# Gate and value products of w_up: one 512-column and one 256-column matmul, folded afterwards, with padded operand rows

## The chip, the cores and the metric

The kernel runs on one core of a Trainium2 chip. The metric is the device time of one execution in microseconds (us). The kernel before takes 1085.06 us, the median of three runs (1084.09 to 1086.23). One execution was recorded by the hardware profiler; the views of that profile are what the prediction argues from.

## The reference

One layer of a streaming encoder on x of shape (1, 256, 2048), all in float32:

```
h = RMSNorm(x);  u = h @ w_in                       # 2048 x 4352
y = concat(short gated conv, Conformer conv (31 taps, LayerNorm), multi-scale pooling)
x = x + RMSNorm(y @ w_out)                          # 2048 x 2048
h = RMSNorm(x)
g, v = causal_conv3(h @ w_up) + bias                # 2048 x 11264, split in two halves of 5632
x = x + RMSNorm((silu(g) * v) @ w_down)             # 5632 x 2048
```

The convolutions run over the 256 tokens, per channel, looking back only.

## The kernel before, in words

**Layout.** Channels lie on the 128 partitions and the T = 256 tokens along the free axis, so that an activation of 2048 channels is KD = 16 row blocks k of 128 x 256. The weights stay in HBM as 364 units of 128 x 1024 floats (68 of w_in, 32 of w_out, 176 of w_up, 88 of w_down), read in one stream by `load` (line 99) into four buffers `raw`.

**Two-part products.** Every operand is split into a high part in the type fp32r and a low part, the rest. For weights, ScalarE copies `raw` to `whi` (`split_hi`, line 108), and VectorE subtracts to get `wlo` (`split_lo`, line 114); each has five buffers. The function `ahead(i)` issues these splits up to AHEAD = 4 units in front of unit i. For activations, `h1`, `y_t` and `h2` have the shape [128, 16, 2, 256]: for each k the 256 high columns, then the 256 low ones, so that one k takes 2,048 bytes of a partition. A product of a weight block with row block k (`product`, line 242) is three matmuls of 256 columns into the same PSUM region: whi with the high part, whi with the low part, wlo with the high part.

**Stages.** In order: the products of w_in with h1 (tiles named in, in_head, in_pool, in_cv, in_b), beside which the mixers run on VectorE, ScalarE and GpSimd (the 31 taps are `acc`, line 379); those of w_out with y_t (tiles o); the second norm, woven into the first products of w_up (tiles up); the rest of w_up (tiles gv); and w_down (tiles d), where the activation parts g_hi and g_lo are the stationary operand and 512 columns of whi or wlo are the moving one (lines 749 to 751).

**Column pairs.** `mm_pair` makes two output columns of 128 channels, one after the other, into the two halves of one PSUM bank: four units, 16 k each, 96 matmuls. In w_up the pair is a gate column j and its value column KF + j, of 44 pairs. The first four pairs come from `mm_group`, which takes eight columns at once along k (tiles up0 to up3, `first[0]` to `first[3]`); the other forty are gv4 to gv43. The PSUM pool has six buffers of one bank.

**The gate.** `gate(j, ps)` scales a pair by the token scale `r2_bc` (VectorE, line 710, PSUM to the SBUF tile `u`), runs the three-tap convolution of each half (`conv3`: ScalarE line 701, VectorE line 703 twice), SiLU on ScalarE (line 712), the product on GpSimd (line 714), and splits the result into g_hi (ScalarE, line 715) and g_lo (VectorE, line 716). Gates 0 to 3 are issued together between the two columns of gv4, gate 4 after gv4, and so on; after gv4 a 128 x 1024 transpose of x follows on VectorE (`transpose_blocks`, line 684).

**Order of the work.** `tick()` counts units; `later(n, fn)` runs fn n units on. The token scales of the second norm come that way: `scales` one unit after the up group, `r2_bc` one more. Each engine works its queue in order. The order within a queue follows the order of the program where operands and buffers allow it, as the framework's own schedule reckons; some instructions are pinned to program order.

**Sum of squares.** In the up stage `square_sum` squares two row blocks at once on ScalarE (line 300), and GpSimd adds the 512 columns to `sum_2` (line 302); small matmuls (line 218) then reduce its two halves over partitions.

Of the kernel before, what the change touches and what calls it, by code (L numbers as in the profile page):

```python
# [8 lines left out]
F32 = mybir.dt.float32  # L9
# [50 lines left out]
UP_ORDER = [x for j in range(KF) for x in (j, KF + j)]  # L60
NATURAL = list(range(KF))

AHEAD = 4
POOL_TAPS = 8

# [4 lines left out]
def trunk_kernel(ctx: ExitStack, tc, xt, vec, g_row, pool_w, w_in, w_out, w_up, w_down, out):  # L70
    nc = tc.nc
    const = ctx.enter_context(tc.tile_pool(name="const", bufs=1))
    units = ctx.enter_context(tc.tile_pool(name="units", bufs=5))
    psum = ctx.enter_context(tc.tile_pool(name="psum", bufs=6, space=bass.MemoryType.PSUM))
    psmall = ctx.enter_context(tc.tile_pool(name="psmall", bufs=2, space=bass.MemoryType.PSUM))
    stat = ctx.enter_context(tc.tile_pool(name="stat", bufs=2))

# [10 lines left out]
    def pin(ins, where=pinned):  # L88
        if where[0]:
            tc.keep_in_program_order(ins)  # L90
# [10 lines left out]
    def split_hi(i, pieces=1):  # L101
        if i not in raws:
            load(i)
        hi = units.tile([P, 1024], F32R, tag="whi", name=f"whi{i}")
        lo = units.tile([P, 1024], F32R, tag="wlo", name=f"wlo{i}")
        parts[i] = (hi, lo)
        for s in cut(pieces):
            pin(nc.scalar.activation(hi[:, s], raws[i][:, s], AF.Copy))  # L108
# [72 lines left out]
    table = const.tile([P, 1], F32, name="table")  # L181
    nc.scalar.activation(table, idle[:, :1], AF.Copy)

    def keep_busy(n):
        warm = psum.tile([P, 512], F32, tag="mm", name="warm")
        for _ in range(n):
            tc.keep_in_program_order(
                nc.tensor.matmul(  # L188
                    warm, idle, idle[:, None, :].to_broadcast([P, 4, P]), start=True, stop=True
                )  # L190
            )
# [3 lines left out]
    def v(name, i):  # L195
        return vec_sb[:, _AT[name] + i : _AT[name] + i + 1]
# [39 lines left out]

    def product(ps, w_hi, w_lo, h, first, last):
        terms = ((w_hi, h[:, 0]), (w_hi, h[:, 1]), (w_lo, h[:, 0]))  # L240
        for n, (w, x) in enumerate(terms):
            nc.tensor.matmul(  # L242
                ps, w, x, start=first and n == 0, stop=last and n == 2, skip_group_check=True
            )

    def bank(name):
        return psum.tile([P, 2, T], F32, tag="mm", name=name)

    def mm_column(u0, ps, ht, opens, order=NATURAL):
        for h in range(2):  # L250
            ahead(u0 + h)
            whi, wlo = parts.pop(u0 + h)
            for kk in range(8):
                k = 8 * h + kk
                c = slice(kk * P, (kk + 1) * P)
                product(ps, whi[:, c], wlo[:, c], ht[:, order[k]], opens and k == 0, k == KD - 1)
            tick()

    def mm_pair(u0, name, ht, order=NATURAL, between=None):
        ps = bank(name)  # L260
        mm_column(u0, ps[:, 0], ht, True, order)
        if between:
            between()
        mm_column(u0 + 2, ps[:, 1], ht, False, order)
        return ps

    def mm_group(u0, name, ht, n, before, order=NATURAL):


        pss = [bank(f"{name}{m}") for m in range(n // 2)]  # L270
        rows = 8 // n
        for u in range(KD // rows):
            for kk in range(rows):
                before(rows * u + kk)
            ahead(u0 + u)
            whi, wlo = parts.pop(u0 + u)
            for kk in range(rows):
                k = rows * u + kk
                for m in range(n):
                    c = slice((kk * n + m) * P, (kk * n + m + 1) * P)  # L280
                    product(
                        pss[m // 2][:, m % 2], whi[:, c], wlo[:, c], ht[:, order[k]],
                        k == 0 and m % 2 == 0, k == KD - 1,
                    )
            tick()
        return pss

    def twice(t):
        return t[:, None, :].to_broadcast([P, 2, T])


    with tc.tile_pool(name="mix", bufs=1) as mix, tc.tile_pool(name="mixt", bufs=2) as mixt:
        h1 = const.tile([P, KD, 2, T], F32R, tag="ht", name="h1")
        sum_x = mix.tile([P, 512], F32, tag="sum", name="sum_x")

        def square_sum(src, total, first, name):
            sq = total
            if not first:
                sq = mixt.tile([P, 512], F32, tag="sq", name=name)
            pin(nc.scalar.activation(sq, src, AF.Square))  # L300
            if not first:
                nc.gpsimd.tensor_tensor(total, total, sq, ALU.add)

        def two(t, kg):
            return t[:, 2 * kg : 2 * kg + 2].rearrange("p k t -> p (k t)")
# [31 lines left out]
        pin(nc.sync.dma_start(pw_sb, pool_w.rearrange("g c d -> c g d")), loading)  # L337
        loading[0] = False

        y_t = mix.tile([P, KD, 2, T], F32R, name="y_t")  # L340
        yo = mix.tile([P, KD, T], F32, name="yo")
        glu6 = mix.tile([P, N_HEADS, T], F32, name="glu6")
        acc6 = mix.tile([P, N_HEADS, 2, T], F32, name="acc6")
# [222 lines left out]
        def out_tiles(m, ps, n=2):  # L566
            sq = sum_y
            if m:
                sq = mixt.tile([P, 2, T], F32, tag="sq", name=f"sqy{m}")
            nc.scalar.activation(sq[:, :n], ps[:, :n], AF.Square)  # L570
            if m:
                nc.gpsimd.tensor_tensor(sum_y[:, :n], sum_y[:, :n], sq[:, :n], ALU.add)
            for j in range(n):
                nc.scalar.activation(
                    yo[:, m + j], ps[:, j], AF.Copy, scale=v("g_post", m + j)
                )
# [20 lines left out]
        for m in range(GROUP_OUT, KD - 2, 2):  # L597
            out_tiles(m, mm_pair(u0, f"o{m}", y_t, OUT_ORDER))
            u0 += 4

        ps = bank("o14")
        mm_column(u0, ps[:, 0], y_t, True, OUT_ORDER)
        out_tiles(KD - 2, ps, 1)
        later(1, most_squares)
        last = bank("o15")
        mm_column(u0 + 2, last[:, 0], y_t, True, OUT_ORDER)
        u0 += 4
        pinned[0] = True
        pin(nc.scalar.activation(last_sq, last[:, 0], AF.Square))
        m_y = stat.tile([P, 2], F32, tag="m2", name="m_y")  # L610
        ps = squares_by_token([last_sq], "y")
        pin(nc.vector.scalar_tensor_tensor(
# [5 lines left out]
        r_y = over_partitions(r, "y")  # L618
        keep_busy(8)
        ahead(u0)  # L620
        pin(nc.scalar.activation(yo[:, KD - 1], last[:, 0], AF.Copy, scale=v("g_post", KD - 1)))

        h2 = const.tile([P, KD, 2, T], F32R, tag="ht", name="h2")
        sum_2 = const.tile([P, 512], F32, name="sum_2")

        def scale_y(kg, ks=None):
            ks = ks or slice(2 * kg, 2 * kg + 2)
# [16 lines left out]
        def elementwise(k):  # L644

            kg, odd = divmod(k, 2)
            if k == 0:
                for j in range(2):
                    scale_y(0, slice(j, j + 1))
                    add_x(0, slice(j, j + 1))  # L650
                    make_lo(j, h2, "g_ffn")
            if not odd:
                if kg < 7:
                    scale_y(kg + 1)
                    add_x(kg + 1)
            else:
                if kg < 7:
                    parts_of(kg + 1)
                square_sum(two(xT, kg), sum_2, kg == 0, f"sq2{kg}")

        first = mm_group(u0, "up", h2, GROUP_UP, weave)
        u0 += 16
# [3 lines left out]
    with tc.tile_pool(name="ffn", bufs=1) as ffn, tc.tile_pool(name="ffnt", bufs=2) as ffnt:  # L666
# [4 lines left out]
        def scales():  # L671
            r_2 = token_rsqrt([sum_2], D, RMS_EPS, "x2")
            later(1, lambda: nc.scalar.activation(r2_bc, over_partitions(r_2, "x2"), AF.Copy))

        later(1, scales)


# [29 lines left out]

        def gate(j, ps):
            u = ffnt.tile([P, 2, T], F32, tag="u", name=f"u{j}")
            nc.vector.tensor_tensor(u, ps, twice(r2_bc), ALU.mult)  # L710
            a = conv3(u[:, 0], j, "cg")
            nc.scalar.activation(a, a, AF.Silu)  # L712
            b = conv3(u[:, 1], KF + j, "cv")
            nc.gpsimd.tensor_tensor(a, a, b, ALU.mult)  # L714
            nc.scalar.activation(g_hi[:, j], a, AF.Copy)
            nc.vector.tensor_tensor(g_lo[:, j], a, g_hi[:, j].bitcast(F32), ALU.subtract)

        n_first = GROUP_UP // 2
        for j in range(n_first, KF):
            ps = mm_pair(  # L720
                u0, f"gv{j}", h2,
                between=(lambda: [gate(i, first[i]) for i in range(n_first)])
                if j == n_first else None,
            )
            u0 += 4
            gate(j, ps)
            if 4 <= j < 28:
                c, at = divmod(j - 4, 6)
                if at == 0:
                    transpose_blocks(c)  # L730
                elif at < 5:
                    move_blocks(c, at - 1)
# [30 lines left out]
        n_kg = KF // 2  # L763
        tail = 4
        for nb in range(4):
            ps = [psum.tile([P, 512], F32, tag="mm", name=f"d{nb}{h}") for h in range(2)]
            for kg in range(n_kg - (tail if nb == 3 else 0)):
                mm_rows(u0 + nb * n_kg + kg, kg, ps)
            if nb < 3:
                for h in range(2):  # L770
                    square_block(nb, h, ps[h])
                    gain_block(nb, h, ps[h])
# [87 lines left out]
```

## Time and profile before

| | |
|---|---|
| median of three runs | 1085.06 us (1084.09 to 1086.23) |
| the profiled execution's own time | 1084.75 us |
| its span, first to last instruction | 1083.0 us, 19157 instructions |
| mean granted TensorE clock | 0.992 |
| DVE share of the span, ACT, POOL | 65%, 50%, 18% |
| HBM traffic over the span | 182 GB/s |

How to read the views: PE is TensorE's matmuls, PEld its weight loads, DVE is VectorE, ACT ScalarE, POOL GpSimd. In a group of instructions stand line, engine, operation, output<-inputs, shapes and count, then busy us and the mean ns of one, then the idle time before them and what ended it. In the chain in order of time stand start, length and what ran, with its count. In a timeline stand start, length, engine, line and operation; a bracket is the idle time before it. In windows, each engine's busy time (and count), then the granted TensorE clock, the DMA share and GB/s.

### The profile page before, as it was taken

How to read it: one execution, taken by the hardware profiler on the slowest of the kernel's cores; microseconds unless marked ns; L12 is line 12 of the kernel's file. 1: busy time of each engine (PE TensorE's matmuls, PEld its weight loads, DVE VectorE, ACT ScalarE, POOL GpSimd, SP SyncE). 2: the span in 40 equal slices, each digit the busy share in tenths (PEclk: the TensorE clock that was granted, in tenths of full speed). 3: DMA queues.
4: the chain of work that ended last, by engine and by line, in shares of the span. 5: the costliest groups of instructions: out<-in, count | busy, mean ns of one | idle time of the engine just before them, and what ended most of it. 6: DMA issues, size and time to landing. Idle time of an engine off the chain costs nothing.

```text
span 1083.0 us, 19157 instructions
## 1 busy us (share of the span) xinstructions
PE 1062.3 (98%) x7761; PEld 1007.5 (93%) x7761; DVE 708.5 (65%) x908; ACT 538.0 (50%) x740; POOL 192.4 (18%) x197
## 2 busy tenths in 40 slices
PE   9999999999999989999999999999999999999996
PEld 7999999999999979999999999999999888888885
DVE  7899988764467757566676766666666444444544
ACT  8745355465546545455454554554554343343431
POOL 4424446421113201011010111111111000000001
PEclk9999999999999989999999999999999999999999
DMA  8645555646545357375664755555556556655552
GB/s 287 202 155 177 179 178 194 208 157 208 185 152 179 116 151 238 115 242 189 174 234 123 250 194 184 185 182 187 179 188 220 193 177 193 193 183 188 193 176 77
DMA packets 73463, 200.00 MB, mean 185 GB/s; under 512 B 23712, under 2 KB 24480, under 8 KB 73248
## 3 DMA queue, kind: packets, MB, share of 16 engines
q1 hardware_dynamic: 73088, 197.72, 56.4%
q8 instruction: 60, 0.98, 0.4%
q10 hardware_dynamic: 288, 1.07, 0.3%
q14 instruction: 27, 0.22, 0.1%
HBM read 194.57 MB, written 2.10 MB: 182 GB/s over the span
## 4 chain that ended last, share of the span: by engine, by line
PE 91%; DVE 6%; issue 1%; ACT 1%; DMA 1%; SPq 0%; DVEq 0%; POOL 0%; ACTq 0%
PE gv L242 43%; PE o L242 8%; PE d L751 8%; PE d L749 8%; PE d L750 8%; PE in_cv L242 6%; PE up L242 4%; DVE acc L379 3%; PE in_b L242 3%; PE in L242 2%; DVE wlo L114 1%; PE in_head L242 1%; DMA raw<-in_w_in 0%; DMA xT<-in_xt 0%; PE warm L188 0%
## 5 line engine op out<-in xcount | busy, mean ns | idle before, releaser
L114 DVE TENSOR_TENSOR wlo<-raw,whi 128x1024 fp32r<-128x1024 f32 (+1 forms) x365 | 450.7, 1239 | 268.6 <-ACT whi L108 266.1
L108 ACT ACTIVATE whi<-raw 128x1024 fp32r<-128x1024 f32 (+1 forms) x365 | 382.7, 1054 | 388.5 <-PE d L751 134.1
L242 PE MATMUL gv<-h,whi 128*128 128x256 f32 x2560 | 463.7, 284 | 4.3 <-ACT whi L108 4.3
L242 PEld LDWEIGHTS gv<-h,whi 128*128 128x128 f32 x2560 | 401.5, 193 | 4.5 <-ACT whi L108 4.5
L242 PE MATMUL gv<-h,wlo 128*128 128x256 f32 x1280 | 363.6, 284 | 1.0 <-DVE wlo L114 1.0
L242 PEld LDWEIGHTS gv<-h,wlo 128*128 128x128 f32 x1280 | 247.1, 193 | 1.2 <-DVE wlo L114 1.2
L749 PE MATMUL d<-whi,g_hi 128*128 128x512 f32 x352 | 139.2, 396 | 0.0
L750 PE MATMUL d<-wlo,g_hi 128*128 128x512 f32 x352 | 139.2, 396 | 0.0
L751 PE MATMUL d<-whi,g_lo 128*128 128x512 f32 x352 | 139.2, 395 | 0.0
L714 POOL TENSOR_TENSOR cg<-cg,cv 128x256 f32<-128x256 f32 x44 | 57.6, 1309 | 413.1 <-ACT cg L712 406.5
L242 PE MATMUL o<-y_t,whi 128*128 128x256 f32 x512 | 91.0, 280 | 0.0
L749 PEld LDWEIGHTS d<-whi,g_hi 128*128 128x128 f32 x352 | 66.2, 188 | 15.9
L751 PEld LDWEIGHTS d<-whi,g_lo 128*128 128x128 f32 x352 | 66.2, 188 | 15.9
L750 PEld LDWEIGHTS d<-wlo,g_hi 128*128 128x128 f32 x352 | 66.2, 188 | 15.9
L242 PEld LDWEIGHTS o<-y_t,whi 128*128 128x128 f32 x512 | 78.2, 188 | 0.1
L242 PE MATMUL o<-y_t,wlo 128*128 128x256 f32 x256 | 71.5, 279 | 0.0
L242 PE MATMUL in_cv<-h,whi 128*128 128x256 f32 x384 | 69.8, 284 | 0.0
L379 DVE SCALAR_TENSOR_TENSOR acc<-glu,vec_sb,acc 128x246 f32<-128x246 f32 (+10 forms) x126 | 66.6, 569 | 2.5 <-POOL acc L402 2.2
L242 PEld LDWEIGHTS in_cv<-h,whi 128*128 128x128 f32 x384 | 60.0, 192 | 0.1
L242 PE MATMUL in_cv<-h,wlo 128*128 128x256 f32 x192 | 54.4, 283 | 0.2 <-DVE wlo L114 0.2
L242 PE MATMUL in_head<-h,whi 128*128 128x256 f32 x256 | 47.9, 289 | 0.0
L242 PEld LDWEIGHTS o<-y_t,wlo 128*128 128x128 f32 x256 | 47.9, 187 | 0.0
(140 smaller groups left out, 1114.7 us busy)
## 6 DMA issues: line engine op xcount, KB each, us to landing
raw<-in_w_up SPq DMA_DIRECT2D x176, 512.0 KB, 3.7
raw<-in_w_down SPq DMA_DIRECT2D x88, 512.0 KB, 4.2
raw<-in_w_in SPq DMA_DIRECT2D x67, 512.0 KB, 4.1
raw<-in_w_out SPq DMA_DIRECT2D x32, 512.0 KB, 4.2
xT<-blocks SPq DMA_DIRECT2D x64, 32.0 KB, 3.6
out<-tail_sb SPq DMA_DIRECT2D x8, 256.0 KB, 2.6
xT<-in_xt SPq DMA_DIRECT2D x7, 256.0 KB, 5.3
tail_sb<-in_g_row ACTq DMA_DIRECT2D x1, 1024.0 KB, 6.0
```

Of the source, the lines that this page charges most:

```text
L108: pin(nc.scalar.activation(hi[:, s], raws[i][:, s], AF.Copy))
L114: pin(nc.vector.tensor_tensor(lo[:, s], raw[:, s], hi[:, s].bitcast(F32), ALU.subtract))
L242: nc.tensor.matmul(ps, w, x, start=first and n == 0, stop=last and n == 2, skip_group_check=True)
L379: nc.vector.scalar_tensor_tensor(a[:, o:], glu[:, : T - o], cb(s), a[:, o:], ALU.mult, ALU.add)
L714: nc.gpsimd.tensor_tensor(a, a, b, ALU.mult)
L749: nc.tensor.matmul(pss[h], g_hi[:, k, s], w1, start=(k == 0), stop=False)
L750: nc.tensor.matmul(pss[h], g_hi[:, k, s], w2, start=False, stop=False)
L751: nc.tensor.matmul(pss[h], g_lo[:, k, s], w1, start=False, stop=(k == KF - 1))
```

## The change

1. *Fused product.* In the gv tiles, `wide_product` replaces the three matmuls of a k: one of 512 columns, whi with both parts of h2, and one of 256, wlo with the high part, into the first 256 columns. A column's sum so stands in two halves of 256 in a whole PSUM bank. The 512-column one comes first, except for the last k.
2. *Fold.* `gate` handles both banks of a gv tile at once: ScalarE copies the second halves (128 x 2 x 256) to `u`, VectorE adds the first halves, and a second VectorE instruction scales in SBUF. The tiles up0 to up3 keep the one scaling.
3. *PSUM.* Three buffers of two banks replace six of one. The two columns of a pair lie in two banks; up and o groups take two pairs per buffer; the last two columns of w_out share one buffer.
4. *First gates.* Gates 0 to 3 are issued 1, 2, 4 and 6 units after `scales`, gate 4 four units after gv4 and gate 5 one unit after gv5.
5. *Pads.* The rows of h1, h2 and y_t get 8 more floats (2,080 bytes instead of 2,048), and so do the buffers of whi and wlo (4,128 instead of 4,096).
6. *Sum of squares.* `sum_2` has 256 columns; GpSimd adds each row block by itself.

```diff
+PAD = 8
-    psum = ctx.enter_context(tc.tile_pool(name="psum", bufs=6, space=bass.MemoryType.PSUM))
+    psum = ctx.enter_context(tc.tile_pool(name="psum", bufs=3, space=bass.MemoryType.PSUM))
...
-        hi = units.tile([P, 1024], F32R, tag="whi", name=f"whi{i}")
-        lo = units.tile([P, 1024], F32R, tag="wlo", name=f"wlo{i}")
+        hi = units.tile([P, 1024 + PAD], F32R, tag="whi", name=f"whi{i}")[:, :1024]
+        lo = units.tile([P, 1024 + PAD], F32R, tag="wlo", name=f"wlo{i}")[:, :1024]
...
+    def banks(name):
+        return psum.tile([P, 2, 512], F32, tag="mm", name=name)
...
+    def wide_product(ps, w_hi, w_lo, h, opens, last):
+        def by_lo():
+            nc.tensor.matmul(ps[:, :T], w_lo, h[:, 0], start=False, stop=False)
+
+        if last:
+            by_lo()
+        nc.tensor.matmul(ps, w_hi, h, start=opens, stop=last)
+        if not last:
+            by_lo()
...
+    def mm_pair(u0, name, ht, order=NATURAL, between=None, wide=False):
+        ps = banks(name)
+        mm_column(u0, ps[:, 0], ht, order, wide)
         if between:
             between()
+        mm_column(u0 + 2, ps[:, 1], ht, order, wide)
+        return ps if wide else ps[:, :, :T]
...
+    def padded(pool, name, **kw):
+
+        t = pool.tile([P, KD, 2 * T + PAD], F32R, name=name, **kw)
+        return t[:, :, : 2 * T].rearrange("p k (j t) -> p k j t", j=2)
...
-        h1 = const.tile([P, KD, 2, T], F32R, tag="ht", name="h1")
+        h1 = padded(const, "h1", tag="ht")
...
-        y_t = mix.tile([P, KD, 2, T], F32R, name="y_t")
+        y_t = padded(mix, "y_t")
...
-        h2 = const.tile([P, KD, 2, T], F32R, tag="ht", name="h2")
-        sum_2 = const.tile([P, 512], F32, name="sum_2")
+        h2 = padded(const, "h2", tag="ht")
+        sum_2 = const.tile([P, T], F32, name="sum_2")
...
-                square_sum(two(xT, kg), sum_2, kg == 0, f"sq2{kg}")
+                sq = mixt.tile([P, 2, T], F32, tag="sq", name=f"sq2{kg}")
+                pin(nc.scalar.activation(sq, xT[:, 2 * kg : 2 * kg + 2], AF.Square))
+                for j in range(2):
+                    a = (sq[:, 0], sum_2)[kg > 0]
+                    if kg or j:
+                        nc.gpsimd.tensor_tensor(sum_2, a, sq[:, j], ALU.add)
...
             later(1, lambda: nc.scalar.activation(r2_bc, over_partitions(r_2, "x2"), AF.Copy))
+
+            for i, n in enumerate((1, 2, 4, 6)):
+                later(n, lambda i=i: gate(i, first[i]))
...
-            nc.vector.tensor_tensor(u, ps, twice(r2_bc), ALU.mult)
+            if ps.shape[-1] == T:
+                nc.vector.tensor_tensor(u, ps, twice(r2_bc), ALU.mult)
+            else:
+                nc.scalar.activation(u, ps[:, :, T:], AF.Copy)
+                nc.vector.tensor_tensor(u, ps[:, :, :T], u, ALU.add)
+                nc.vector.tensor_tensor(u, u, twice(r2_bc), ALU.mult)
...
-            ps = mm_pair(
-                u0, f"gv{j}", h2,
-                between=(lambda: [gate(i, first[i]) for i in range(n_first)])
-                if j == n_first else None,
-            )
+            ps = mm_pair(u0, f"gv{j}", h2, wide=True)
             u0 += 4
-            gate(j, ps)
+            if j == n_first:
+                later(4, lambda ps=ps: gate(n_first, ps))
+            elif j == n_first + 1:
+                later(1, lambda ps=ps: gate(n_first + 1, ps))
+            else:
+                gate(j, ps)
...
-            ps = [psum.tile([P, 512], F32, tag="mm", name=f"d{nb}{h}") for h in range(2)]
+            pair = banks(f"d{nb}")
+            ps = [pair[:, h] for h in range(2)]
```

More of the change, by code (lines that the diff above doesn't have):

```diff
@@ L182, in trunk_kernel @@
     nc.scalar.activation(table, idle[:, :1], AF.Copy)
+    def banks(name):
+        return psum.tile([P, 2, 512], F32, tag="mm", name=name)
     def keep_busy(n):
-        warm = psum.tile([P, 512], F32, tag="mm", name="warm")
+        warm = banks("warm")[:, 0]
         for _ in range(n):
@@ L235, in over_partitions, with product @@
         return ps[:, :T]
-    def product(ps, w_hi, w_lo, h, first, last):
+    def product(ps, w_hi, w_lo, h, opens, last):
         terms = ((w_hi, h[:, 0]), (w_hi, h[:, 1]), (w_lo, h[:, 0]))
@@ L242, in product, with mm_column @@
             nc.tensor.matmul(
-                ps, w, x, start=first and n == 0, stop=last and n == 2, skip_group_check=True
+                ps, w, x, start=opens and n == 0, stop=last and n == 2, skip_group_check=True
             )
-    def bank(name):
-        return psum.tile([P, 2, T], F32, tag="mm", name=name)
-    def mm_column(u0, ps, ht, opens, order=NATURAL):
+    def wide_product(ps, w_hi, w_lo, h, opens, last):
[6 more added lines that the diff above has]
+            by_lo()
+    def mm_column(u0, ps, ht, order=NATURAL, wide=False):
         for h in range(2):
@@ L255, in mm_column @@
                 c = slice(kk * P, (kk + 1) * P)
-                product(ps, whi[:, c], wlo[:, c], ht[:, order[k]], opens and k == 0, k == KD - 1)
+                args = (whi[:, c], wlo[:, c], ht[:, order[k]], k == 0, k == KD - 1)
+                if wide:
+                    wide_product(ps, *args)
+                else:
+                    product(ps[:, :T], *args)
             tick()
-    def mm_pair(u0, name, ht, order=NATURAL, between=None):
-        ps = bank(name)
-        mm_column(u0, ps[:, 0], ht, True, order)
+    def mm_pair(u0, name, ht, order=NATURAL, between=None, wide=False):
+        ps = banks(name)
+        mm_column(u0, ps[:, 0], ht, order, wide)
         if between:
             between()
-        mm_column(u0 + 2, ps[:, 1], ht, False, order)
-        return ps
+        mm_column(u0 + 2, ps[:, 1], ht, order, wide)
+        return ps if wide else ps[:, :, :T]
     def mm_group(u0, name, ht, n, before, order=NATURAL):
-        pss = [bank(f"{name}{m}") for m in range(n // 2)]
+        pss = []
+        for m in range(n // 4):
+            ps = banks(f"{name}{m}")
+            pss += [ps[:, j].rearrange("p (j t) -> p j t", j=2) for j in range(2)]
         rows = 8 // n
@@ L599, in trunk_kernel @@
             u0 += 4
-        ps = bank("o14")
-        mm_column(u0, ps[:, 0], y_t, True, OUT_ORDER)
-        out_tiles(KD - 2, ps, 1)
+        ps = banks("o14")
+        mm_column(u0, ps[:, 0], y_t, OUT_ORDER)
+        out_tiles(KD - 2, ps[:, :1, :T], 1)
         later(1, most_squares)
-        last = bank("o15")
-        mm_column(u0 + 2, last[:, 0], y_t, True, OUT_ORDER)
+        last = ps[:, 1, :T]
+        mm_column(u0 + 2, ps[:, 1], y_t, OUT_ORDER)
         u0 += 4
         pinned[0] = True
-        pin(nc.scalar.activation(last_sq, last[:, 0], AF.Square))
+        pin(nc.scalar.activation(last_sq, last, AF.Square))
         m_y = stat.tile([P, 2], F32, tag="m2", name="m_y")
@@ L620, in trunk_kernel @@
         ahead(u0)
-        pin(nc.scalar.activation(yo[:, KD - 1], last[:, 0], AF.Copy, scale=v("g_post", KD - 1)))
-        h2 = const.tile([P, KD, 2, T], F32R, tag="ht", name="h2")
-        sum_2 = const.tile([P, 512], F32, name="sum_2")
+        pin(nc.scalar.activation(yo[:, KD - 1], last, AF.Copy, scale=v("g_post", KD - 1)))
+        h2 = padded(const, "h2", tag="ht")
+        sum_2 = const.tile([P, T], F32, name="sum_2")
         def scale_y(kg, ks=None):
@@ L719, in trunk_kernel @@
         for j in range(n_first, KF):
-            ps = mm_pair(
-                u0, f"gv{j}", h2,
-                between=(lambda: [gate(i, first[i]) for i in range(n_first)])
-                if j == n_first else None,
-            )
-            u0 += 4
-            gate(j, ps)
+            ps = mm_pair(u0, f"gv{j}", h2, wide=True)
+            u0 += 4
+            if j == n_first:
+                later(4, lambda ps=ps: gate(n_first, ps))
+            elif j == n_first + 1:
+                later(1, lambda ps=ps: gate(n_first + 1, ps))
+            else:
+                gate(j, ps)
             if 4 <= j < 28:
```

## The prediction

> **What bounds the kernel now.** I read the page first: busy shares, the chain that ended last, the costliest groups.
>
> ```profile
> PE 1062.3 (98%) x7761; PEld 1007.5 (93%) x7761; DVE 708.5 (65%) x908; ACT 538.0 (50%) x740; POOL 192.4 (18%) x197
> PE 91%; DVE 6%; issue 1%; ACT 1%; DMA 1%; SPq 0%; DVEq 0%; POOL 0%; ACTq 0%
> L242 PE MATMUL gv<-h,whi 128*128 128x256 f32 x2560 | 463.7, 284 | 4.3 <-ACT whi L108 4.3
> L242 PE MATMUL gv<-h,wlo 128*128 128x256 f32 x1280 | 363.6, 284 | 1.0 <-DVE wlo L114 1.0
> L749 PE MATMUL d<-whi,g_hi 128*128 128x512 f32 x352 | 139.2, 396 | 0.0
> ```
>
> TensorE makes up 91% of the chain, and the gate and value tiles (gv) that the change rewrites are 3840 of its 7761 matmuls. The 284 ns of a record overlap the next record, so the price of a matmul is the distance between starts. The chain in order of time gives that as stretch divided by count:
>
> ```profile
> 144.64 23.04 PE in_cv L242 x192
> 234.87 69.61 PE o L242 x591
> 309.25 1.73 PE warm L188 x8
> 310.98 46.17 PE up L242 x384
> 360.02 0.79 PE ss_x L218 x8
> 387.38 440.41 PE gv L242 x3646
> ```
>
> A 256-column product costs 120.0 ns with h1 or h2 as the moving operand (23.04/192; up 46.17/384 = 120.2; gv 440.41/3646 = 120.8) and 117.8 ns with y_t (69.61/591). A bf16 512-column filler costs 216 ns (1.73/8). The only fp32r products of 512 columns are those of w_down; their timeline from 900 us, first and last of 23 consecutive starts:
>
> ```profile
> 899.72 0.40 PE L749 MATMUL d<-whi,g_hi 128*128 128x512 f32 x1
> ...
> 904.85 0.40 PE L750 MATMUL d<-wlo,g_hi 128*128 128x512 f32 x1
> ```
>
> 5.13 us over 22 steps is 233.2 ns. Next the gv stage (357 to 827 us) in windows:
>
> ```profile
> core 0: us, PE busy (x) PEld busy (x) DVE busy (x) ACT busy (x) POOL busy (x), PEclk, DMA share, GB/s
> 381.00:387.40 6.40, 1.03 (x8) 0.62 (x6) 5.05 (x8) 2.76 (x5) 1.74 (x2) 0.94 0.01 2
> 387.40:391.00 3.60, 3.60 (x17) 3.60 (x18) 2.09 (x3) 2.31 (x3) 0.51 (x1) 0.50 0.48 73
> 391.00:600.00 209.00, 209.00 (x1735) 209.00 (x1735) 137.31 (x182) 104.32 (x142) 22.37 (x17) 0.99 0.62 192
> 600.00:827.00 227.00, 227.00 (x1894) 227.00 (x1893) 151.28 (x199) 116.66 (x159) 28.42 (x20) 1.00 0.60 193
> ```
>
> From 391 us on TensorE never stops (1894 matmuls in 227 us, 119.9 ns each), so a shorter spacing shortens the stage one to one. The one hole lies at 381 to 387.4. VectorE's timeline shows its cause:
>
> ```profile
> 368.98 1.22 DVE L114 TENSOR_TENSOR wlo<-raw,whi 128x1024 fp32r<-128x1024 f32 x1
> 370.12 0.68 DVE L710 TENSOR_TENSOR u<-up,r_bc 128x512 f32<-128x512 f32 x1
> ...
> 384.58 1.24 DVE L684 STREAM_TRANSPOSE blocks<-xT 128x1024 f32<-128x1024 f32 x1
> ...
> 386.10 1.22 DVE L114 TENSOR_TENSOR wlo<-raw,whi 128x1024 fp32r<-128x1024 f32 x1
> ```
>
> Between 370.2 and 386.1 us VectorE runs gates 0 to 3 and the next ones back to back and not one weight split (wlo), so the lead of four units runs out. TensorE loses 6.40 - 1.03 = 5.4 us, and about 0.5 us more at the edges of what it did run. Then the granted clock is 0.50 for 3.6 us: 17 records where 3.6/0.120 = 30 would fit, and with the missing records counted I take 2.4 us. Together about 8.3 us.
>
> **Fused product.** Per product, three matmuls of 256 columns (360 ns) become one of 512 and one of 256; the columns streamed stay 768, one weight load of three goes. There are 40 tiles x 2 columns x 16 k = 1280 products. Nearest rows: 233.2 for the wide one, 117.8 to 120 for the narrow one; I take 118: rows of h are 2,048 bytes and weight buffers 4,096 apart, and in the layout before they all start at one place modulo 512 bytes (y_t 320 bytes off it); with the pads they spread in steps of 32. Pair 351.2, saving 8.8 ns, times 1280 = **-11.3 us**, all on the path. Bounds: nothing, if the wide one costs 2 x 120; and the filler's rate, 216 + 108 = 324, which gives -46 us.
>
> **Fold.** Each gv gate gains a ScalarE copy and a VectorE add out of PSUM, and its scaling now reads SBUF twice. Prices, from the groups by form (those of 357 to 827 us first, then the whole span):
>
> ```profile
> L114 DVE TENSOR_TENSOR wlo<-raw,whi 128x1024 fp32r<-128x1024 f32 x160 | 195.1, 1225 | 85.9 <-ACT whi L108 84.0
> L108 ACT ACTIVATE whi<-raw 128x1024 fp32r<-128x1024 f32 x160 | 167.1, 1053 | 137.5 <-PE gv L242 102.6 <-DMA raw<-in_w_up 32.6 <-PE up L242 1.2
> L714 POOL TENSOR_TENSOR cg<-cg,cv 128x256 f32<-128x256 f32 x43 | 56.2, 1306 | 403.0 <-ACT cg L712 396.4 <-DVE cv L703 6.6
> L710 DVE TENSOR_TENSOR u<-gv,r_bc 128x512 f32<-128x512 f32 x39 | 26.9, 690 | 27.0 <-PE gv L242 27.0
> L701 ACT ACTIVATE cg<-u,vec_sb 128x256 f32<-128x256 f32 x43 | 25.4, 591 | 29.0 <-DVE u L710 28.8 <-DVE g_lo L716 0.2
> L703 DVE SCALAR_TENSOR_TENSOR cg<-u,vec_sb,cg 128x255 f32<-128x255 f32 x43 | 20.9, 487 | 2.8 <-ACT cg L701 2.7
> L716 DVE TENSOR_TENSOR g_lo<-cg,g_hi 128x256 fp32r<-128x256 f32 x43 | 18.2, 424 | 39.1 <-ACT g_hi L715 39.1
> L715 ACT ACTIVATE g_hi<-cg 128x256 fp32r<-128x256 f32 x43 | 17.9, 417 | 57.7 <-POOL cg L714 57.7
> L712 ACT ACTIVATE cg<-cg 128x256 f32<-128x256 f32 x43 | 17.4, 405 | 6.6 <-DVE cg L703 6.6
> L570 ACT ACTIVATE sqy<-o 128x512 f32<-128x512 f32 x6 | 3.6, 608 | 0.0
> L633 DVE TENSOR_TENSOR xT<-xT,yo 128x512 f32<-128x512 f32 x7 | 6.8, 969 | 0.2
> ```
>
> VectorE per tile now: 4 splits x 1.22 + 0.69 + four taps x 0.48 + 0.42 = 7.9 us in 96 x 0.120 = 11.5 us. After: + 0.97 for the second pass (both operands in SBUF, as in L633; 0.69 if it costs what one from PSUM does) = 8.9 us in 32 x 0.351 = 11.2 us, 79%. ScalarE: 4 x 1.05 + 2 x 0.59 + 0.41 + 0.42 = 6.2, + 0.61 = 6.8 us, 61%. What queues behind the new wait on ScalarE's copy is the next unit's split, and that has four units (11.2 us) of lead. Cost **0**, covered by that lead and 2.3 us of VectorE slack per tile; the price when the cover goes is the slower rival below.
>
> **Three double banks for six single ones.** A gv tile waits for the gate three tiles earlier, two tiles or 22 us back; the fold chain up to the last PSUM read is under 2 us. In the other stages the splits already tie VectorE and ScalarE to within four units of TensorE. 0. The last two w_out columns now share a double bank that the up group may reuse, after the ScalarE copy of column 15; ScalarE makes h2's first rows behind that copy anyway. 0.
>
> **First gates spread out.** Units 2 to 12 (28 us) must hold on VectorE gates 0 to 5 (4 x 3.0 + 2 x 4.0), ten splits (12.2) and a transpose (1.2): 33.5 us, 5.5 over, and with one 0.9 us wait per gate (39.1/43) some 11 over, against a lead of 11.2 less the 2.3 that one split takes on its way (1.05 + 1.22). I leave 3 of the 8.3 us: **-5.3 us** (0 to -8.3). What is late next: gate 3's PSUM read before tile gv6, within those 3.
>
> **Sum of squares.** sum_2 folds to 256 columns: 4 small matmuls for 8, half of 0.79, **-0.4 us**. POOL does two short adds per pair of rows for one long; it idles 4 us between pairs there:
>
> ```profile
> 344.43 1.76 POOL L302 TENSOR_TENSOR sum<-sum,sq 128x512 f32<-128x512 f32 x1 [4.01 <-ACT sq L300]
> ```
>
> At the price of L714 two are 2.6 us for 1.76; hidden.
>
> **Pads elsewhere.** Where h is the moving operand and TensorE sets the pace (up, 384, and the in stage from 118 us on, some 800), 120 may become 118: -2.4 us; before 118 us the chain runs over VectorE's acc taps, nothing. The o products may lose up to 2.2 ns x 768 = 1.7 us, and d is as likely to gain as to lose. I take **-1 us** (-2.4 to +4). The Trainium skill (SBUF — State Buffer, "SBUF: two separate sides") says that TensorE's port waits for no other engine; by that rule this term is 0 and the sum 1068. No row here separates its own two reads, but 120.0 against 117.8 ns for one shape in two tiles shows that something in the operands' place matters.
>
> **Sum.** The profiled execution took 1084.75 us (span 1083.0), 0.3 under the median of 1085.06. 1084.75 - 11.3 - 5.3 - 0.4 - 1 = 1066.8; against the median **1067 us**.
>
> **Rivals.**
> 1. Only the fixed part of an instruction is saved. 2 x 117.8 - 233.2 = 2.4 ns is what one 512 saves over two 256; if the 120-class rate stays with the columns, the gain is 2.4 x 1280 = 3.1 us: 1084.75 - 3.1 - 5.3 - 0.4 = **1076**. For it: the same rows give both readings. Against: the pads move just the operands that were slow. The Trainium skill (TensorE: Matmul & The Clock Gate, "Back-to-back issue gap") has the warm spacing as N/2.4 + 2.5 ns; by it a product goes from 327.5 to 325, so the estimate is 3.2 us. Its level disagrees with this trace (109 ns against 120), its fixed part fits 2.4.
> 2. The excess belongs to the weight load. At granted clock 0.50 the spacing is 0.64/3 = 213 ns:
>
> ```profile
> 387.75 0.63 PE L242 MATMUL gv<-h,whi 128*128 128x256 f32 x2
> ...
> 388.39 0.63 PE L242 MATMUL gv<-h,whi 128*128 128x256 f32 x2
> ```
>
> Half is 106.7, so 120 carries 13.3 ns; one load fewer saves 13.3 x 1280 = 17 us: **1061**. Against: d carries 233.2 - 213.4 = 20 for a single load.
> 3. The pads remove the whole fp32r excess, the filler's rate everywhere: -46 in gv, -18 in d (17 x 1056), -7 in o, -14 in in and up: near **995**. No fp32r row comes near it.
> 4. Slower: VectorE becomes the bound in gv. If a gate ran unbroken in its queue, it would hold it for 0.61 + 0.69 + 0.97 + 0.59 + 1.94 + 0.41 + 1.31 + 0.42 + 0.42 = 7.4 us, plus four splits 4.9 = 12.3 us per tile; 40 x 12.3 = 490 for the stage's 470: **1105**. It decides from 11.2 us per tile on and makes the kernel slower from about 11.7. Against: now the same reckoning gives 10.7, yet the queue puts splits into the gaps and a gate shows 0.9 us of waiting; 8.9 + 0.9 + 0.6 = 10.4.
>
> **How the numbers follow.** Forecast 0.55 (own range 1060 to 1073), rival 1 0.20, rival 2 0.07, rival 3 0.06, rival 4 0.08, and 0.04 that leftovers cancel. Leaving out 3, 4 and the edges, the range is 1054 to 1080. Faster by over 0.2% (about what runs of this kernel can tell): 0.55 + 0.20 + 0.07 + 0.06 = 0.88; within 0.04; slower 0.08.
>
> **What would show it.** In the profile after: gv 512-column starts about 233 ns before the next, narrow ones 118; per gv tile 11.2 us; splits between the first gates, no 5 us hole after 381 us and no half clock there; ss_x x4; VectorE near 79% in gv with TensorE unbroken. I am wrong if the wide spacing is 240, or if wlo waits stop TensorE in gv.

## The result and the profile after

The changed kernel takes **1067.78 us**, median of four runs (1066.56 to 1068.78), against 1085.59 for the kernel before beside it (1084.09 to 1086.23): ratio 0.9837, interval 0.982 to 0.9854, so 1.6% faster. Forecast: 1067, within 1054 to 1080.

The page after, the lines that answer to those of before:

```profile
PE 1044.7 (98%) x6477; PEld 933.7 (88%) x6477; DVE 730.8 (69%) x948; ACT 560.0 (53%) x780; POOL 200.7 (19%) x205
L257 PE MATMUL gv<-h,whi 128*128 128x512 f32 x1280 | 443.4, 394 | 1.5 <-DVE u L743 1.5
L253 PE MATMUL gv<-h,wlo 128*128 128x256 f32 x1280 | 346.2, 281 | 0.0
```

TensorE still fills 98% of a shorter span, with 1284 matmuls fewer: 1280 in gv and 4 in the sum of squares. The rate in gv is read where TensorE never stops in either kernel, 400 to 800 us, as windows. Before (time, PE busy and count, PEld, DVE, ACT, POOL):

```profile
400.00:800.00 400.00, 400.00 (x3335) 400.00 (x3335) 267.47 (x354) 204.74 (x281) 47.95 (x35) 1.00 0.60 192
```

After:

```profile
400.00:800.00 400.00, 400.00 (x2283) 349.56 (x2283) 294.74 (x400) 229.31 (x324) 52.93 (x37) 1.00 0.62 192
```

A product was three matmuls: 3 x 400/3335 = 359.8 ns. It is now two: 2 x 400/2283 = 350.4 ns. That is 9.4 ns, times 1280 products 12.0 us.

From the first matmul of a stage to the first of the next, us (o ends with its last product, d with its last matmul; the differences are of the unrounded times):

| stage | before | after | difference |
|---|---|---|---|
| up to the in products | 4.7 | 4.8 | +0.1 |
| in | 208.9 | 209.2 | +0.3 |
| o | 92.6 | 94.9 | +2.3 |
| second norm | 4.6 | 4.6 | 0 |
| up | 46.2 | 45.8 | -0.4 |
| gv | 470.6 | 451.3 | -19.3 |
| d | 246.2 | 246.5 | +0.4 |
| after the last matmul | 9.2 | 8.7 | -0.5 |
| span | 1083.0 | 1065.9 | -17.1 |

So gv gave 19.3 us: 12.0 by the rate, 0.4 by the four small matmuls, and the rest, 6.9, by the hole that closed. The start of gv in windows, before:

```profile
357.00:391.00 34.00, 28.63 (x225) 28.22 (x224) 25.38 (x45) 18.27 (x32) 7.73 (x8) 0.94 0.25 71
```

and after:

```profile
357.00:391.00 34.00, 32.53 (x196) 28.63 (x195) 26.59 (x39) 20.20 (x31) 7.27 (x7) 1.00 0.63 179
```

TensorE was idle 5.4 of these 34 us and at a mean clock of 0.94; now it is idle 1.5 at 1.00. But three stops stand in the timeline after that the kernel before did not have:

```profile
302.34 0.51 PE L247 MATMUL o<-y_t,whi 128*128 128x256 f32 x2 [1.67 <-ACT yo L599]
...
373.09 0.47 PE L257 MATMUL gv<-h,whi 128*128 128x512 f32 x1 [1.47 <-DVE u L743]
...
1051.80 0.50 PE L787 MATMUL d<-whi,g_hi 128*128 128x512 f32 x1 [1.62 <-DVE tail_sb L799]
```

The bracket names who ended the wait: ScalarE's read of column 14 of w_out ahead of column 15, VectorE's read of up1 ahead of gv5, VectorE's read of the first half of the last w_down block ahead of its second half. By the distance of starts they cost about 1.8, 1.6 and 1.8 us.

### The profile page after: what moved, and what is told of

Its sections match the earlier page's. It is cut to its first block, busy times and chain, and to the rows that moved or that the text cites. A ratio compares the mean times of both kernels' runs of the same rounds, so it can differ in the third digit from the quotient of the medians.

```text
span 1065.9 us, 16675 instructions
## 1 busy us (share of the span) xinstructions
PE 1044.7 (98%) x6477; PEld 933.7 (88%) x6477; DVE 730.8 (69%) x948; ACT 560.0 (53%) x780; POOL 200.7 (19%) x205
## 4 chain that ended last, share of the span: by engine, by line
PE 90%; DVE 5%; issue 1%; DMA 1%; ACT 1%; SPq 0%; DVEq 0%; POOL 0%; ACTq 0%
PE gv L257 28%; PE gv L253 14%; PE o L247 9%; PE d L787 8%; PE d L789 8%; PE d L788 8%; PE in_cv L247 6%; PE up L247 4%; DVE acc L404 3%; PE in_b L247 3%; PE in L247 2%; DVE wlo L115 1%; DMA raw<-in_w_in 1%; PE in_head L247 1%; ACT whi L109 0%
## 5 line engine op out<-in xcount | busy, mean ns | idle before, releaser
L257 PE MATMUL gv<-h,whi 128*128 128x512 f32 x1280 | 443.4, 394 | 1.5 <-DVE u L743 1.5
L253 PE MATMUL gv<-h,wlo 128*128 128x256 f32 x1280 | 346.2, 281 | 0.0
L257 PEld LDWEIGHTS gv<-h,whi 128*128 128x128 f32 x1280 | 235.0, 188 | 51.4 <-ACT whi L109 1.8
L253 PEld LDWEIGHTS gv<-h,wlo 128*128 128x128 f32 x1280 | 240.7, 188 | 6.8
L751 POOL TENSOR_TENSOR cg<-cg,cv 128x256 f32<-128x256 f32 x44 | 62.0, 1411 | 390.0 <-ACT cg L749 358.3
L745 ACT ACTIVATE u<-gv 128x512 f32<-128x512 f32 x40 | 23.8, 594 | 57.7 <-PE gv L257 57.7
L746 DVE TENSOR_TENSOR u<-gv,u 128x512 f32<-128x512 f32 x40 | 27.5, 688 | 36.4 <-ACT u L745 36.4
```

The source lines that it names most:

```text
L253: nc.tensor.matmul(ps[:, :T], w_lo, h[:, 0], start=False, stop=False)
L257: nc.tensor.matmul(ps, w_hi, h, start=opens, stop=last)
L745: nc.scalar.activation(u, ps[:, :, T:], AF.Copy)
L746: nc.vector.tensor_tensor(u, ps[:, :, :T], u, ALU.add)
```

## The experiments

**Three narrow products.** The gv products go back to three matmuls, and with them the fold goes; all else stays.

```diff
-            ps = mm_pair(u0, f"gv{j}", h2, wide=True)
+            ps = mm_pair(u0, f"gv{j}", h2)
```

> The changed kernel with the gv products back at three matmuls of 256 columns and the gate without the fold; double banks, spread gates, pads and the short sum stay. The gv stage of the changed kernel lasts 451.3 us, 350.6 ns per product once its 1.7 us stop and the small matmuls are taken off. Theory 'width': one instruction fewer makes the gain, a pad does nothing for a 256-column product, so three cost 360 ns again and gv is 12 us longer: about 1080 us. Theory 'place': most of the gain is that with pads the operands no longer start at one place, so three narrow ones cost 354 ns and gv is 4.4 us longer: about 1072 us.

1071.28 us, ratio to before 0.9873 (0.9858 to 0.9888). Its window:

```profile
400.00:800.00 400.00, 400.00 (x3384) 400.00 (x3383) 270.81 (x360) 206.67 (x285) 49.54 (x37) 1.00 0.61 191
```

A padded narrow matmul costs 400/3384 = 118.2 ns where it cost 119.9; three cost 354.6. Fusing alone is then worth 4.2 ns per product, 5.4 us. The time rises by only 3.5: this kernel has no stop at gv5 (1.6 us), so that its gv lasts 455.1 us for 451.3, and in the two traces its in stage is 1.5 us shorter than the changed kernel's.

**No pads.**

```diff
-PAD = 8
+PAD = 0
```

> The changed kernel with pads of 0 bytes; the fused product and all else stay. Theory 'width': the wide product costs the 233 ns of w_down wherever it starts, the narrow one 120: 353 ns, gv 3 us longer, up and in about 2 us longer: about 1072 us. Theory 'place': at the common place the wide one costs 2 x 120 - 2.4 = 237.6, pair 357.6, gv 9 us longer, with up and in: about 1079 us. In the timeline the spacing after a wide matmul is 233 or 238.

1073.64 us, ratio 0.9897 (0.988 to 0.9913).

```profile
400.00:800.00 400.00, 400.00 (x2266) 346.92 (x2265) 293.04 (x400) 229.00 (x324) 53.01 (x37) 1.00 0.62 190
```

Pair: 2 x 400/2266 = 353.0 ns, near the 353 of "width" and far from the 357.6 of "place". But the parts are those of neither theory. In the timeline stand the first and the last of 13 pairs and the start after them:

```profile
600.26 0.40 PE L257 MATMUL gv<-h,whi 128*128 128x512 f32 x1
600.49 0.28 PE L253 MATMUL gv<-h,wlo 128*128 128x256 f32 x1
...
604.50 0.40 PE L257 MATMUL gv<-h,whi 128*128 128x512 f32 x1
604.73 0.28 PE L253 MATMUL gv<-h,wlo 128*128 128x256 f32 x1
604.85 0.40 PE L257 MATMUL gv<-h,whi 128*128 128x512 f32 x1
```

The mean distance from one start to the next, from 400 to 800 us, is 236.2 ns after a wide matmul and 117.1 after a narrow one, where "width" had 233 and 120. With both pads it is 232.2 and 118.4. So in this pair the pads act on the wide matmul, and a narrow one at the common place costs 117.1 ns beside a wide one where it costs 120 among narrow ones. From 359.8, fusing without pads takes 6.8 and the pads 2.6 more; or the pads take 5.2 first and fusing 4.2. The pads also shorten up by 0.6 us and d by 1.5 (gv 3.4). For d the windows 815 to 1040 us show it, with 972 matmuls for 966:

```profile
815.00:1040.00 225.00, 225.00 (x972) 182.03 (x971) 104.44 (x94) 89.97 (x96) 1.48 (x1) 1.00 0.62 189
```

is the changed kernel, and without pads

```profile
815.00:1040.00 225.00, 225.00 (x966) 180.34 (x965) 105.59 (x97) 91.37 (x98) 1.49 (x1) 1.00 0.61 193
```

**Pads on one side.** Two kernels: pads on the weight buffers alone, and on the rows of h1, h2 and y_t alone.

```diff
-        t = pool.tile([P, KD, 2 * T + PAD], F32R, name=name, **kw)
+        t = pool.tile([P, KD, 2 * T], F32R, name=name, **kw)
```

> The changed kernel with pads on the buffers of whi and wlo alone; rows of h1, h2, y_t unpadded. With both pads a gv pair costs 350.7 ns and the stage 451.3 us, with none 353.4 and 454.7. Theory: what counts is the place of the moving rows relative to the weights, so either pad alone gives most of it: gv 451 to 452.5 us, 1068 to 1070 us. Rival: the moving row's own place counts, and then this run stays at 454.7 us in gv, 1072 us or more.

```diff
-        hi = units.tile([P, 1024 + PAD], F32R, tag="whi", name=f"whi{i}")[:, :1024]
-        lo = units.tile([P, 1024 + PAD], F32R, tag="wlo", name=f"wlo{i}")[:, :1024]
+        hi = units.tile([P, 1024], F32R, tag="whi", name=f"whi{i}")[:, :1024]
+        lo = units.tile([P, 1024], F32R, tag="wlo", name=f"wlo{i}")[:, :1024]
```

> The changed kernel with pads on the rows of h1, h2, y_t alone. Theory of the relative place: gv 451 to 452.5 us, w_down (which has no padded row) back at 248.1 us, 1069 to 1070 us. Rival, the weights' own place counts: gv 454.7 us, 1072 us or more.

1067.77 us (0.9835, 0.9821 to 0.9848) and 1068.75 us (0.9845, 0.9831 to 0.9858). Weights alone:

```profile
400.00:800.00 400.00, 400.00 (x2281) 349.53 (x2280) 294.87 (x400) 229.22 (x323) 52.83 (x37) 1.00 0.64 192
```

Rows alone:

```profile
400.00:800.00 400.00, 400.00 (x2283) 348.83 (x2282) 294.19 (x400) 230.26 (x324) 52.87 (x37) 1.00 0.63 192
```

Either pad alone brings the pair to 350.4 to 350.7 ns, and w_down, whose operands have no padded row, keeps its gain only with padded weights (246.6 and 248.1 us). So neither operand needs pads of its own: padding one of the two is enough. That fits the theory that their relative place counts, but no run varies the offset, and the 117.1 ns of the run without pads shows that place is not all.

**Gates together.**

```diff
-            for i, n in enumerate((1, 2, 4, 6)):
-                later(n, lambda i=i: gate(i, first[i]))
...
-            ps = mm_pair(u0, f"gv{j}", h2, wide=True)
+            ps = mm_pair(
+                u0, f"gv{j}", h2, wide=True,
+                between=(lambda: [gate(i, first[i]) for i in range(n_first)])
+                if j == n_first else None,
+            )
             u0 += 4
-            if j == n_first:
-                later(4, lambda ps=ps: gate(n_first, ps))
-            elif j == n_first + 1:
-                later(1, lambda ps=ps: gate(n_first + 1, ps))
-            else:
-                gate(j, ps)
+            gate(j, ps)
```

> The changed kernel with gates 0 to 3 issued together between the two columns of gv4, and gates 4 and 5 right after their tiles, as before the change. Theory: the hole of before and the half clock after it come from the gates standing ahead of the weight splits, so both return, 8.3 us for the 1.7 that are left now: about 1074.5 us, with a stop of 4 us or more in gv and a window at clock 0.50. Rival: the schedule spreads them anyway now that each gate waits for its buffers: within 1 us of 1068, no half clock.

1079.14 us, ratio 0.9948 (0.9933 to 0.9962): the hole is back and larger, 11.4 us slower than the changed kernel where 6.6 were expected.

```profile
365.00:383.80 18.80, 18.46 (x107) 15.83 (x105) 14.28 (x29) 10.12 (x19) 4.93 (x5) 1.00 0.28 85
383.80:393.00 9.20, 0.94 (x3) 0.29 (x2) 7.73 (x14) 5.06 (x10) 2.22 (x3) 0.73 0.01 1
393.00:398.40 5.40, 5.40 (x17) 4.63 (x18) 2.79 (x3) 2.31 (x3) 0.53 (x1) 0.51 0.58 132
```

TensorE stands for 8.3 us of 383.8 to 393 and then runs 5.4 us at a mean clock of 0.51. In this kernel's VectorE timeline no weight split stands between

```profile
369.93 1.23 DVE L115 TENSOR_TENSOR wlo<-raw,whi 128x1024 fp32r<-128x1024 f32 x1 [1.48 <-ACT whi L109]
...
391.73 1.22 DVE L115 TENSOR_TENSOR wlo<-raw,whi 128x1024 fp32r<-128x1024 f32 x1
```

20.6 us apart, where it was 15.9 before. Between them VectorE scales four up tiles where it scaled two before, works the fold's extra pass for two gv tiles (1.4 us) and waits 2.2 us for ScalarE. So the fold makes the same bad order dearer, but not alone.

**The kernel before, with its gates spread.** The same lines the other way, on the kernel before.

```diff
+            for i, n in enumerate((1, 2, 4, 6)):
+                later(n, lambda i=i: gate(i, first[i]))
...
-            ps = mm_pair(
-                u0, f"gv{j}", h2,
-                between=(lambda: [gate(i, first[i]) for i in range(n_first)])
-                if j == n_first else None,
-            )
+            ps = mm_pair(u0, f"gv{j}", h2)
             u0 += 4
-            gate(j, ps)
+            if j == n_first:
+                later(4, lambda ps=ps: gate(n_first, ps))
+            elif j == n_first + 1:
+                later(1, lambda ps=ps: gate(n_first + 1, ps))
+            else:
+                gate(j, ps)
```

> The kernel before with nothing but the first gates spread out (six single banks, narrow products, no pads). Theory: the hole at 381 to 387 us and the half clock after it come from the order of the gates alone; without the fold there is less to place and no double bank to wait for, so all of the 8.3 us go: gv from 470.6 to about 462.5 us, 1077 us. Rival: part of the gain in the changed kernel comes from the fused product's shorter weight stream or the banks, and a stop of 2 us or more remains: 1079 us or more.

1077.56 us, ratio 0.9924 (0.9908 to 0.9941); gv takes 462.1 us for 470.6.

```profile
357.00:391.00 34.00, 34.00 (x287) 34.00 (x286) 26.46 (x39) 19.27 (x30) 8.53 (x6) 1.00 0.59 166
```

No idle time and full clock: the order of the gates alone made the hole, and 8.5 us is its price.

**No fold.** The gates read only the first half of each bank, which leaves the products with the low part of h2 out of the result; the matmuls are the same.

```diff
-            ps = mm_pair(u0, f"gv{j}", h2, wide=True)
+            ps = mm_pair(u0, f"gv{j}", h2, wide=True)[:, :, :T]
```

> The changed kernel whose gates read only the first 256 columns of each bank (ScalarE copy and second VectorE pass are left out, and with them the part of the result that the low half of h2 gives); the matmuls are the same. Theory: the fold is covered, VectorE goes from 74% to about 67% of gv and the time stays at 1068 us, within 0.7 us. Rival: VectorE's load already holds TensorE back here and there: 2 us or more faster.

1067.03 us, ratio 0.9834 (0.9819 to 0.9849). gv takes 451.3 us with and without; the traces differ in the in stage (208.5 us for 209.2), which lay between 207.7 and 209.8 over all these traces.

```profile
400.00:800.00 400.00, 400.00 (x2284) 349.60 (x2283) 270.84 (x364) 209.61 (x288) 49.62 (x36) 1.00 0.62 192
```

VectorE falls from 294.7 to 270.8 busy us and TensorE gains one matmul in 2284. The fold costs TensorE nothing.

**Own banks.** Column 15 of w_out and each half of the last w_down block get their own double bank.

```diff
-        last = ps[:, 1, :T]
-        mm_column(u0 + 2, ps[:, 1], y_t, OUT_ORDER)
+        last_ps = banks("o15")
+        last = last_ps[:, 0, :T]
+        mm_column(u0 + 2, last_ps[:, 0], y_t, OUT_ORDER)
...
-            pair = banks(f"d{nb}")
-            ps = [pair[:, h] for h in range(2)]
+            if nb < 3:
+                pair = banks(f"d{nb}")
+                ps = [pair[:, h] for h in range(2)]
+            else:
+                ps = [banks(f"d{nb}{h}")[:, 0] for h in range(2)]
```

> As the run before it, but with the transposes where the changed kernel has them: the two stops by a shared double bank go, 3.6 us less than the changed kernel, 1064.2 us. Rival: a stop only moves, because a third buffer is not yet free there: 1066 or more.

1063.07 us, ratio 0.9791 (0.9778 to 0.9805). The windows at the two places, changed kernel:

```profile
299.00:304.00 5.00, 3.33 (x29) 3.13 (x28) 2.28 (x2) 1.69 (x3) 1.45 (x1) 1.00 0.53 192
1044.00:1056.00 12.00, 10.38 (x45) 8.12 (x44) 4.11 (x6) 1.42 (x3) 2.30 (x2) 1.00 0.18 68
```

Own banks:

```profile
297.00:302.00 5.00, 5.00 (x44) 5.00 (x43) 2.45 (x2) 2.37 (x4) 1.30 (x2) 1.00 0.67 206
1040.00:1052.00 12.00, 12.00 (x53) 9.73 (x52) 5.08 (x6) 1.41 (x3) 2.32 (x2) 1.00 0.13 46
```

Both stops are gone; o is 92.9 us for 94.9 and d 244.7 for 246.5, together 3.8 us. The time fell by 4.7 where 3.6 was expected: in this trace the in stage is 0.9 us shorter as well, for which there is a reason below (pads elsewhere).

**Own banks and late transposes.** The same, and

```diff
-            if 4 <= j < 28:
-                c, at = divmod(j - 4, 6)
+            if 8 <= j < 32:
+                c, at = divmod(j - 8, 6)
```

> The changed kernel, where column 15 of w_out and each half of the last w_down block get a double bank of their own, and the four transposes of x come four tiles later. Three stops stand in the trace of the changed kernel: 1.8 us before column 15 (it waits for ScalarE's last read of column 14 in the same double bank), 1.8 us before the second half of the last w_down block (VectorE's read of the first half), 1.6 us at gv5 (gate 1's PSUM read, behind a transpose). Theory: waits go by the whole double bank, so the first two stops vanish, and the third shrinks by the transpose's 1.2 us: 4.8 us less, 1063.0 us. Rival: the reader's bank is not the cause and PE waits there for something else (the weight split, ScalarE's queue): 1067 to 1068.

1063.01 us, ratio 0.9792 (0.9779 to 0.9805). The stop at gv5 shrinks and gv falls from 451.4 to 450.2 us, as reckoned, but in this trace the in stage is 1.05 us longer than with own banks; the two times are the same. That the expected 1063.0 was met is luck: the in stage was not in that reckoning. Both are faster than the changed kernel by 0.4%, and the fastest measured here.

## Why the prediction was right, step by step

- *Fused product, -11.3 predicted, -12.0 measured.* Right: the wide matmul starts 232.2 ns before the next (233.2 in w_down), the narrow one 118.4 (118 taken), and the pair came out at 350.4 for 351.2. The reason was right in part: the pads were to bring the narrow matmul from 120 to 118, but without them it is the wide one that costs more, 236.2, and the narrow one 117.1. Rival 1 (2.4 ns per product, 1076 us) falls: without pads the saving is 6.8 ns, with them 9.4. The Trainium skill (TensorE: Matmul & The Clock Gate, "Back-to-back issue gap") has 2.5 ns per instruction, for the gap of an isolated matmul; the 4.2 ns of fusing on padded operands is the nearest the runs came to it. Rival 2 (346.7 per pair) falls too. Rival 3 falls: pads are worth 1.7 ns of a matmul's 119.9, not the whole excess.
- *Fold, 0.* Right, shown by leaving it out. VectorE stands at 294.7/400 = 74%, not 79%: the second pass took 0.70 us rather than L633's 0.97, worth 2.4 points, and the same sum of means was 2 points too high for the kernel before too (7.9 of 11.5 us is 69%, its window has 67%). Rival 4 never came near.
- *First gates, -5.3 predicted, about -6.9 measured.* The mechanism is shown by two runs. The hole's price was 8.5 us by the spread gates of the kernel before, near the 8.3 of the prediction, whose account of the half clock was wrong: it lasted 6.0 us, not 3.6, and no records are missing (gv has all 3840).

```profile
387.40:393.40 6.00, 6.00 (x28) 6.00 (x29) 2.79 (x3) 2.35 (x4) 0.51 (x1) 0.50 0.63 137
```

28 matmuls where 6.0/0.120 = 50 fit is a loss of 2.6 us, for the 2.4 taken. The rest of the hole is 1.6 us, not 3, and what is late is gate 1's read ahead of gv5, behind a transpose, not gate 3's ahead of gv6.
- *Sum of squares, -0.4.* As reckoned.
- *Three double banks, 0.* **This step failed.** The prediction followed buffers from tile to tile, and asked of the shared w_out bank only what the tile after it waits for. A double bank is one tile, and in this program the matmuls into one half wait for a reader of the other: column 15 waits for the reads of column 14, the second w_down half for those of the first. By the distance of starts that is 3.6 us; with banks of their own o and d are 3.8 us shorter.
- *Pads elsewhere, -1.* About -1.9 in up and d together (in the table d's 1.5 is hidden by its stop), +0.4 in o (92.93 us with own banks for 92.56 before), but the in stage returned nothing. Up to the pool products near 117 us the faster matmuls only wait longer. Windows before

```profile
107.00:118.00 11.00, 9.66 (x77) 9.20 (x77) 11.00 (x17) 4.98 (x8) 6.61 (x9) 1.00 0.44 145
118.00:124.00 6.00, 6.00 (x51) 5.95 (x50) 6.00 (x12) 3.15 (x5) 1.73 (x4) 1.00 0.66 205
150.00:210.00 60.00, 60.00 (x503) 60.00 (x502) 48.68 (x63) 32.09 (x46) 34.46 (x32) 1.00 0.59 192
```

and after

```profile
107.00:118.00 11.00, 8.95 (x74) 8.54 (x72) 11.00 (x15) 5.26 (x8) 6.89 (x9) 0.97 0.41 117
118.00:124.00 6.00, 6.00 (x37) 5.64 (x38) 6.00 (x12) 2.91 (x4) 1.24 (x3) 0.76 0.64 237
150.00:210.00 60.00, 60.00 (x509) 60.00 (x509) 48.90 (x63) 32.48 (x47) 35.06 (x32) 1.00 0.59 193
```

have VectorE busy all the time in the first stretch in both. Beyond 118 us the forecast counted on about 1.6 us. The shorter spacing is there, 509 matmuls for 503 in 60 us, but just after the pool products the granted clock is 0.76 for 6 us. From the first pool product to the first of o it is 96.4 us before and 96.2 after. In the traces of own banks, no fold, three narrow products and pads on the rows, the clock does not fall there (with own banks 118 to 124 us has x50 at 1.00), and the same stretch takes 95.3 us: 1.1 us of the gain came. Why the clock falls in some traces is open: with pads on the rows TensorE waits as long just before.

So the sum, 16.8 by its own time for the forecast's 18, was right with a missed cost of 3.6 us, most of which larger gains paid for: 0.7 in the fused product, 1.6 in the first gates. That the forecast of 1067 came within 1 us of the measured time is luck in so far as these errors cancelled.

## What to carry to other kernels

Where matmuls run back to back, price them by the distance of their starts, from rows of the same type and width; a busy time that overlaps says nothing. When PSUM tiles are merged into larger ones, list for every merged tile who still reads one half while the other is to be written. And when a batch of late work is issued at once, compare its length on the splitting engine with the lead of the stream that shares its queue: here 16 us against 11 cost some 8.5 us, over a quarter of it by the clock that fell afterwards.

## What the runs showed of the hardware

The spacing of fp32r matmuls moves with where the moving operand and the weights lie: among matmuls of 256 columns it was 119.9 ns with both at one common place modulo 512 bytes and 118.2 on average over places 32 bytes apart, and shifting either operand was enough. It also moves with the neighbours: at that common place a matmul of 256 columns cost 117.1 ns beside one of 512, which cost 236.2. The Trainium skill (SBUF — State Buffer, "SBUF: two separate sides") says that TensorE's port never waits on anyone; it speaks of engines among each other. The effect here does not look like another engine's: in the kernel before, the starts from 400 to 800 us are 120 ns apart throughout (one is 119), whatever the other engines do. No run here shows why, and no single best offset was looked for.

The granted clock fell to 0.50 after TensorE had stood 4.6 and then 1.3 us (the kernel before, for 6.0 us, 213 ns per matmul of 256 columns), and for some 5.4 us after stops of 7.9 and 1.5 us (gates together). The stop of 1.6 us at gv5 in the changed kernel left it at 1.00; two waits of about 1 us each at the pool products were followed by 0.76 in the changed kernel and by 1.00 with pads on the rows.
